# Moving five layer-1 blocks and twelve gathers from a PEER loop into the end of its gate matrix

## The chip, the cores and the metric

The kernel runs on one core of a Trainium2 chip. The metric is the device time of one execution in microseconds (us), lower is better. TensorE is called PE here, VectorE DVE, ScalarE ACT, GpSimd POOL and SyncE SP.

## The reference

One encoder block on 512 tokens of width 1024: normalisation, a combined projection, neighbourhood attention and grouped-query attention, gated merge, residual; then PEER, a retrieval of single-neuron experts; then a last normalisation. The change touches PEER alone:

```python
def peer(xn, w_q, sub_keys, u, v):
    q = (xt @ w_q).reshape(t, PEER_HEADS, 2, PEER_HALF)
    sc = jnp.einsum("thpc,hpnc->thpn", q, sub_keys)
    top_s, top_i = lax.top_k(sc, PEER_TOPK)
    ...
    best_s, best_pos = lax.top_k(cand_s, PEER_TOPK)
    idx = jnp.take_along_axis(cand_i, best_pos, axis=-1)
    gate = jax.nn.softmax(best_s, axis=-1)
    ...
        uc = u[ic]
        act = jnp.einsum("cd,ced->ce", xc, uc)
        hid = jax.nn.gelu(act, approximate=False) * gc
        return jnp.einsum("ce,ced->cd", hid, v[ic])
```

Each token has 8 heads x 16 experts = 128 of the 16384 experts, whose rows of `u` and `v` are 1024 float32 wide.

## The kernel before

The 512 tokens are four tiles of 128. For the first two tiles and half of the third (T1 = 320 tokens) the kernel doesn't gather: it computes all 16384 experts densely, in NK = 128 blocks of 128 experts, and multiplies by a gate matrix that is zero where an expert wasn't chosen. For the other half of the third tile (64 tokens, "X") the products with `u` are gathered row by row, NX = 64 gathers of 128 rows, and the resulting hidden values go through the gate matrix too. The fourth tile (GA) is gathered altogether: P = 128 gathers of u and 128 of v.

A *layer-1 block* (`layer1`, L610) loads one block of `u` (512 KB), splits it into a high part (ACT, `whi`, L82) and a low part (`wlo`, L84, on DVE or POOL), and makes 24 matmuls of 320 columns (L100 to L102) and a Gelu into a tile `ge` of 128 x 320. A *layer-2 block* (`layer2`, L898) makes 18 matmuls of 512 columns (L905) from the hidden values `hh`, `hl` of one block and the split block of `v`, and accumulates in PSUM. `hidden` (L881) multiplies `ge` by the block's gates and splits the product.

The *gate matrix* (L819 to L861) is made from token groups: 96 groups of 4 tokens. For each group DVE writes one-hot tiles `oh` (L838), ACT (odd groups, L844) or POOL (even groups, L846) scales them by the gates, PE multiplies four pairs (L850), and ACT evicts the result into `stg` (L851). Four groups make a chunk, which SP writes to DRAM (`gdram`, L859). The last 16 groups, from group 80 on, need the hidden values of the X half tile: `hx` is transposed on PE and copied to `pk` (L829, L830). Between the groups stand the gathers of X (`gather_x`) and layer-1 blocks.

NB = 47 layer-1 blocks are done ahead of the loop and their `ge` kept in SBUF (pool `blp`): 21 before the gate matrix, NG = 17 spread over the first 80 groups, NP = 5 ahead of `hx`'s transpose, and 4 behind the last gate matmul.

The *loop* (L964) has one step per block: split the next block of v (`vget`), take or make the next block's `ge` (`get_ge`: kept for j < 47, else a layer-1 block in the loop), `hidden`, `layer2`, and some gathers of tile GA (`gather_to`), whose pace is set by `gw`: a step without layer 1 counts 1, one with it 2.25. A gather of u is an indirect DMA that POOL issues (L626, kept in program order) and a multiplication with row sums on DVE (L629); in the X gathers the second factor, `xgx`, lies in PSUM, in those of tile GA, `xg`, in SBUF. A gather of v is an indirect DMA (L634) and a multiply-add on DVE (L637). The pools have few buffers: `raw` 3, `whi` and `wlo` 4 each, `oh` 5, the gather pool of X (`gatx`) 4, those of the loop (`gat`) 3 for u and 3 for v.

The order on each engine is fixed at build time by a planner that simulates the program; `issue_after` keeps an instruction behind another in that simulation.

Of the kernel before, what the change touches and what calls it, by code (L numbers as in the profile page):

```python
# [11 lines left out]
F32 = mybir.dt.float32  # L12
# [10 lines left out]
P = 128  # L23
# [6 lines left out]
NK = 128  # L30
# [3 lines left out]
TD = ND * P  # L34
HB = P // 2
T1 = TD - HB
NB = 47
CH = 16
GJ = 8
NX = 64  # L40
NEG = -1.0e30
WSTART = (0, 64, 192, 256)
KIND = (1, 0, 0, 2)
# [5 lines left out]
def tile_block(ctx, tc, x, out, g1, g2, gfr, gq, gk, w_in, w_a, w_b, w_o, w_q,  # L49
               rpb, keys, u_rows, u_blk, v_blk, rope_c, rope_s, mask, iota):  # L50
    nc = tc.nc
    mm = nc.tensor.matmul
    act = nc.scalar.activation
    vec = nc.vector
# [63 lines left out]
    dp = ctx.enter_context(tc.tile_pool(name="dp", bufs=1, space=DRAM))  # L118
    bdram = dp.tile([H, P, 512], F32, name="bdram")
    gdram = dp.tile([P, TD // CH, P * CH], F32, name="gdram")  # L120
    xdram = dp.tile([ND, P, D], F32, name="xdram")
    def rstd_int(ss, shape, width, p, tag):
        m = p.tile(shape, F32, name="rm" + tag)
        vec.tensor_scalar(out=m, in0=ss, scalar1=1.0 / width, scalar2=EPS, op0=ALU.mult, op1=ALU.add)
        r = p.tile(shape, F32, name="rr" + tag)
        t = p.tile(shape, F32, name="rt" + tag)
        vec.tensor_copy(out=t, in_=m.bitcast(I32))
        vec.tensor_scalar(out=r.bitcast(I32), in0=t, scalar1=-0.5, scalar2=1597463007.0,
                          op0=ALU.mult, op1=ALU.add)
        vec.tensor_scalar(out=m, in0=m, scalar1=-0.5, scalar2=None, op0=ALU.mult)  # L130
        for _ in range(4):
            vec.tensor_tensor(out=t, in0=r, in1=r, op=ALU.mult)
            vec.tensor_tensor(out=t, in0=t, in1=m, op=ALU.mult)
            vec.scalar_tensor_tensor(out=r, in0=t, scalar=1.5, in1=r, op0=ALU.add, op1=ALU.mult)
        return r
# [47 lines left out]
    with ExitStack() as pa:  # L183
# [329 lines left out]
        xg = xa.tile([P, D], F32, name="xg")  # L513
# [83 lines left out]
    codeU = gp.tile([P, P], I32, name="codeU")  # L597
# [12 lines left out]
    def layer1(j, keep, eng):  # L610
        uh, ul = load_split(u_blk[j], eng)
        ps = psm.tile([P, S], F32, name="ps_mm")
        last_l1[0] = acc3(ps[:, :T1], [(uh[:, k * P:(k + 1) * P], ul[:, k * P:(k + 1) * P],
                                        xah[:, k], xal[:, k]) for k in range(KD)])
        ge = keep.tile([P, T1], F32, name="ge")
        with tc.issue_after(last_hi[0].ins) if j < 2 else ExitStack():
            act(ge, ps[:, :T1], AF.Gelu)  # L617
        return ge

    u_src = u_rows  # L620
# [23 lines left out]
    def gather_to(goal):  # L644
        while sum(npu) < min(goal, 2 * P):
            pu, pv = npu
            if pu < P and pu - pv < 32:
                gather_u(pu, gat, codeU, xg, actg)
                npu[0] += 1
                if npu[0] % 16 == 0:  # L650
                    act_g(pu // 16)
            else:
                gather_v(pv)
                npu[1] += 1
# [3 lines left out]
    with pb:  # L658
# [85 lines left out]

        def backlog(n, eng=vec):
            for _ in range(n):
                if nbl[0] < NB:
                    gelu_bl.append(layer1(nbl[0], blp, eng))
                    nbl[0] += 1

# [3 lines left out]
        def gather_x(goal):  # L754
            while len(stt) < min(goal, NX):
                stt.append(gather_u(len(stt), gatx, codeX, xgx, actx))
# [57 lines left out]
        ngr = T1 // 4 - 8  # L814
        nx0 = len(stt)
        gms = []
        NP = 5
        NG = NB - 4 - NP - nbl[0]
        for ch in range(TD // CH):  # L819
            if ch == T1 // CH - 1:  # L820
                act(actx, actx, AF.Gelu)
                for o, z in ((HB, 0), (0, 1)):
                    vec.tensor_tensor(out=hsel(hx[HB:], z), in0=hcol(actx[o:o + HB]),
                                      in1=hcol(gateX[o:o + HB]), op=ALU.mult)
            if ch == T1 // CH:
                with tc.issue_after(gms[-1].ins):
                    backlog(NP, pool)
                with tc.issue_after(last_l1[0].ins):
                    nc.tensor.transpose(pst[:, :P], hx, ident)  # L829
                vec.tensor_copy(out=ijg[GX][:, 2, HB:], in_=pst[:, HB:P])  # L830
            stg = stp.tile([P, P, CH], F32, name="stg", bufs=3)
            for t4 in range(CH // 4):
                t = ch * CH + t4 * 4
                pk = ijg[t // P]
                c = t % P
                oh = stp.tile([P, 2, 4, P], F32, name="oh", bufs=5)
                with tc.issue_after(stt[max(0, len(stt) - 4)].ins):
                    vec.tensor_tensor(out=oh,  # L838
                                      in0=iops.unsqueeze(1).unsqueeze(1).broadcast_to([P, 2, 4, P]),
                                      in1=pk[:, 0:2, c:c + 4].unsqueeze(3).broadcast_to([P, 2, 4, P]),  # L840
                                      op=ALU.is_equal)
                if t4 % 2:
                    for z in range(4):
                        act(oh[:, 0, z], oh[:, 0, z], AF.Copy, scale=pk[:, 2, c + z:c + z + 1])  # L844
                else:
                    pool.tensor_tensor(out=oh[:, 0], in0=oh[:, 0],  # L846
                                       in1=pk[:, 2, c:c + 4].unsqueeze(2).broadcast_to([P, 4, P]), op=ALU.mult)
                ps = psb.tile([P, S], F32, name="ps_s", bufs=3)
                for z in range(4):
                    gm = mm(ps[:, z * P:(z + 1) * P], oh[:, 0, z], oh[:, 1, z], start=True, stop=True)  # L850
                act(stg[:, :, t4 * 4:t4 * 4 + 4].rearrange("p j t -> p t j"),  # L851
                    ps.rearrange("p (t j) -> p t j", t=4), AF.Copy)
                gms.append(gm)
                g = t // 4
                gather_x(nx0 + (NX - nx0) * (g + 1) // ngr)
                if g and NG * min(g + 1, T1 // 4) // (T1 // 4) > NG * min(g, T1 // 4) // (T1 // 4):
                    with tc.issue_after(gms[-2].ins):
                        backlog(1, (vec, pool)[nbl[0] % 2])
            nc.sync.dma_start(gdram[:, ch], stg.rearrange("p j t -> p (j t)"))  # L859
        with tc.issue_after(gm.ins):  # L860
            backlog(NB, vec)  # L861
        px.close()

    psd = ctx.enter_context(tc.tile_pool(name="psd", bufs=1, space=PSUM, reuse_waits="tile"))
# [56 lines left out]
    ge = {}  # L921

    def get_ge(j):
        return gelu_bl[j] if j < NB else layer1(j, dq, vec)

    def finish(tt):
        if tt == GA:
# [32 lines left out]
    vget = lambda j: load_split(v_blk[j], vec, dq)  # L960
    vnx = vget(0)
    nxt = hidden(0, get_ge(0))
    gw = (2 * P) / (NB + 2.25 * (NK - NB - 5))
    for j in range(NK - 1):  # L964
        cur, vcur = nxt, vnx
        vnx = vget(j + 1)
        nxt = hidden(j + 1, get_ge(j + 1))
        if j < NK - 2:
            layer2(j, cur, vcur)
        with tc.issue_after(nxt[2].ins):  # L970
            gather_to(int(gw * (min(j + 1, NB) + 2.25 * max(0, j + 1 - NB))))
    tc.keep_in_program_order(act(warm, warm, AF.Sqrt))
    finish(GA)
    layer2_last((cur, nxt), (vcur, vnx))
# [80 lines left out]
```

## Time and profile before

| | us |
|---|---|
| median of 3 runs | 1695.64 (1693.13 to 1696.81) |
| profiled execution, its own time | 1703.01 |
| its span, first to last instruction | 1701.1 |
| PE busy | 1603.3 |
| DVE busy | 1296.4 |
| ACT busy | 810.1 |
| POOL busy | 776.1 |

Times in the trace count from the start of the span. A busy PE is not PE at its peak: matmuls are pipelined and their ends are modelled, so the distance of their starts is the better measure. A view of groups sums instructions of one line; a window sums each engine over a stretch; the chain of waits follows the work that ended last back from release to release; the timeline shows instructions in order, with the idle time before each in brackets and what ended it.

### The profile page before, as it was taken

The page shows a single profiled execution, that of the slowest core. Times are in us where ns is not written, and L with a number is a line of the kernel's source. Part 1 is how long each engine was busy: PE and PEld are TensorE (multiplying, and loading weights), DVE is VectorE, ACT ScalarE, POOL GpSimd, SP SyncE. Part 2 cuts the span into 40 slices and gives each one's busy share as a digit, 9 for nine tenths or more (in the row PEclk, how much of TensorE's full clock was granted, in tenths as well). Part 3 has the DMA queues.
Part 4 walks back from the last instruction along what each step waited for, and adds up shares of the span by engine and source line. Part 5 has one row for each costly group of instructions (what it writes and reads, how often), then busy time and mean ns, then how long its engine had stood idle before and what let it go on. Part 6 is the DMA issues. An engine that isn't in the chain of part 4 may idle for free.

```text
span 1701.1 us, 25989 instructions
## 1 busy us (share of the span) xinstructions
PE 1603.3 (94%) x9390; PEld 1439.8 (85%) x9390; DVE 1296.4 (76%) x2595; ACT 810.1 (48%) x1523; POOL 776.1 (46%) x653
## 2 busy tenths in 40 slices
PE   8999999998999868889889999999999999999997
PEld 7888988788999758779878888989898989888986
DVE  7266766536799889997568877888888888888875
ACT  5446566434333358787634434443434344434334
POOL 2543221123688977676213433444444445443341
PEclk9989999999999979999999999999999999999999
DMA  7523221323222559997589999999999999999882
GB/s 249 147 57 92 80 70 50 103 91 125 95 94 92 198 190 343 340 341 272 207 271 338 331 326 315 324 338 334 347 345 336 341 350 332 344 347 311 305 304 106
DMA packets 162482, 407.44 MB, mean 240 GB/s; under 512 B 21297, under 2 KB 72881, under 8 KB 159282
## 3 DMA queue, kind: packets, MB, share of 16 engines
q1 hardware_dynamic: 114848, 235.63, 40.2%
q0 software_dynamic: 47360, 169.89, 28.6%
q8 instruction: 74, 1.21, 0.3%
q14 instruction: 54, 0.44, 0.1%
q10 hardware_dynamic: 146, 0.27, 0.0%
HBM read 374.02 MB, written 30.87 MB: 238 GB/s over the span
## 4 chain that ended last, share of the span: by engine, by line
PE 67%; DVE 12%; DMA 8%; ACT 5%; POOL 4%; issue 4%; SPq 0%; DVEq 0%; POOLq 0%; ACTq 0%
PE acc L905 27%; PE ps_mm L100 11%; PE ps_mm L102 11%; PE ps_mm L101 11%; DMA vg<-in_v_blk_dram,codeV 2%; DMA ug<-in_u_rows_dram,codeX 2%; PE ps_s L850 1%; ACT stg L851 1%; POOL wlo L84 1%; DMA raw<-in_v_blk_dram 1%; ACT whi L82 1%; PE ps_o L100 1%; PE ps_o L102 1%; PE ps_o L101 1%; DVE codes L741 1%
## 5 line engine op out<-in xcount | busy, mean ns | idle before, releaser
L82 ACT ACTIVATE whi<-raw 128x1024 fp32r<-128x1024 f32 x322 | 341.4, 1061 | 474.6 <-PE ps_mm L101 202.9
L84 DVE TENSOR_TENSOR wlo<-raw,whi 128x1024 fp32r<-128x1024 f32 x234 | 287.0, 1229 | 144.4 <-ACT whi L82 127.0
L100 PE MATMUL ps_mm<-xah,whi 128*128 128x320 f32 x1152 | 361.7, 314 | 7.5 <-ACT ge L617 5.8
L102 PE MATMUL ps_mm<-xah,wlo 128*128 128x320 f32 x1152 | 359.6, 312 | 6.3 <-POOL wlo L84 3.6
L101 PE MATMUL ps_mm<-xal,whi 128*128 128x320 f32 x1152 | 358.6, 311 | 0.0
L84 POOL TENSOR_TENSOR wlo<-raw,whi 128x1024 fp32r<-128x1024 f32 x88 | 213.1, 2423 | 288.7 <-ACT whi L82 249.6
L626 POOL DMA_INDIRECT ug<-in_u_rows_dram,codeU x128 | 159.1, 1243 | 261.7 <-DVE ug L629 241.8
L634 POOL DMA_INDIRECT vg<-in_v_blk_dram,codeV x128 | 177.6, 1387 | 219.7 <-DVE yg L637 197.4
L905 PE MATMUL acc<-whi,hh 128*128 128x512 f32 x756 | 243.3, 397 | 4.4 <-ACT hh L90 4.4
L905 PE MATMUL acc<-wlo,hh 128*128 128x512 f32 x756 | 239.6, 397 | 0.0
L905 PE MATMUL acc<-whi,hl 128*128 128x512 f32 x756 | 235.0, 395 | 0.0
L100 PEld LDWEIGHTS ps_mm<-xah,whi 128*128 128x128 f32 x1152 | 218.4, 190 | 12.8 <-ACT ge L617 7.2
L102 PEld LDWEIGHTS ps_mm<-xah,wlo 128*128 128x128 f32 x1152 | 218.2, 189 | 8.9 <-POOL wlo L84 4.4
L101 PEld LDWEIGHTS ps_mm<-xal,whi 128*128 128x128 f32 x1152 | 218.4, 190 | 3.6
L637 DVE SCALAR_TENSOR_TENSOR yg<-vg,hidg,yg 128x1024 f32<-128x1024 f32 x128 | 164.2, 1283 | 11.3 <-DMA vg<-in_v_blk_dram,codeV 11.1
L905 PEld LDWEIGHTS acc<-wlo,hh 128*128 128x128 f32 x756 | 142.5, 188 | 34.5
L905 PEld LDWEIGHTS acc<-whi,hl 128*128 128x128 f32 x756 | 142.0, 188 | 34.3
L905 PEld LDWEIGHTS acc<-whi,hh 128*128 128x128 f32 x756 | 139.0, 188 | 32.4 <-ACT hh L90 5.3
L629 DVE SCALAR_TENSOR_TENSOR ug<-ug,xg 128x1024 f32<-128x1024 f32 x128 | 155.7, 1219 | 0.0
L850 PE MATMUL ps_s<-oh 128*128 128x128 f32 x768 | 108.7, 294 | 33.1 <-POOL oh L846 20.0
L850 PEld LDWEIGHTS ps_s<-oh 128*128 128x128 f32 x768 | 100.5, 200 | 39.8 <-POOL oh L846 25.9
L90 ACT ACTIVATE hh<-hd 128x384 fp32r<-128x384 f32 x128 | 66.8, 522 | 140.2 <-DVE hd L892 115.8
(278 smaller groups left out, 2879.8 us busy)
## 6 DMA issues: line engine op xcount, KB each, us to landing
raw<-in_u_blk_dram SPq DMA_DIRECT2D x128, 512.0 KB
raw<-in_v_blk_dram SPq DMA_DIRECT2D x128, 512.0 KB
gdram<-stg SPq DMA_DIRECT2D x24, 1024.0 KB
gtl<-gdram SPq DMA_DIRECT2D x64, 384.0 KB
raw<-in_w_in_dram SPq DMA_DIRECT2D x34, 512.0 KB
raw<-in_w_q_dram SPq DMA_DIRECT2D x16, 512.0 KB
x_t<-in_x_dram SPq DMA_DIRECT2D x8, 512.0 KB
raw<-in_w_o_dram SPq DMA_DIRECT2D x8, 512.0 KB
```

Of the source, the lines that this page charges most:

```text
L82: act(hi, raw, AF.Copy)
L84: eng.tensor_tensor(out=lo, in0=raw, in1=hi.bitcast(F32), op=ALU.subtract)
L90: last_hi[0] = act(hi, src, AF.Copy, scale=scale)
L100: mm(ps, ah, bh, start=i == 0, stop=False)
L101: mm(ps, ah, bl, start=False, stop=False)
L102: last = mm(ps, al, bh, start=False, stop=i == n - 1)
L626: i_ = pool.indirect_dma_start(out=t, out_offset=None, in_=u_src, in_offset=bass.IndirectOffsetOnAxis(ap=code[:, p:p + 1], axis=0))
L629: return vec.scalar_tensor_tensor(out=t, in0=t, scalar=1.0, in1=mul, op0=ALU.mult, op1=ALU.mult, accum_out=dst[:, p:p + 1])
L634: i_ = pool.indirect_dma_start(out=t, out_offset=None, in_=v_src, in_offset=bass.IndirectOffsetOnAxis(ap=codeV[:, p:p + 1], axis=0))
L637: vec.scalar_tensor_tensor(out=yg, in0=t, scalar=hidg[:, p:p + 1], in1=yg, op0=ALU.mult, op1=ALU.add)
L850: gm = mm(ps[:, z * P:(z + 1) * P], oh[:, 0, z], oh[:, 1, z], start=True, stop=True)
L905: mm(accs[tt][hf], st_[:, ts_], mv[:, hf * S:(hf + 1) * S], start=j == 0 and st_ is hh and mv is vh, stop=False)
```

## The change

Five more blocks (NS = 5, numbers 47 to 51) get their layer 1 ahead of the loop. Their `ge` is written to DRAM (`sdram`) by ACT's queue and loaded again in the loop by SP's, two steps ahead. Of the 52 blocks NP = 6 stand ahead of `hx`'s transpose and NA = 8 behind the last gate matmul. NE = 12 gathers of u for tile GA are issued with the last 12 gate groups, 84 to 95, through the X gathers' pool; the loop's pace counts them as done.

```diff
+NS = 5
+NE = 12
...
+    sdram = dp.tile([NS, P, T1], F32, name="sdram")
...
-        ge = keep.tile([P, T1], F32, name="ge")
+        spill = NB <= j < NB + NS
+        ge = stp.tile([P, T1], F32, name="sge", bufs=2) if spill else keep.tile([P, T1], F32, name="ge")
         with tc.issue_after(last_hi[0].ins) if j < 2 else ExitStack():
             act(ge, ps[:, :T1], AF.Gelu)
+        if spill:
+            nc.scalar.dma_start(sdram[j - NB], ge)
...
-                if nbl[0] < NB:
+                if nbl[0] < NB + NS:
...
-        NP = 5
-        NG = NB - 4 - NP - nbl[0]
+        NP = 6
+        NA = 8
+        NG = NB + NS - NA - NP - nbl[0]
...
                 gather_x(nx0 + (NX - nx0) * (g + 1) // ngr)
+                if g >= TD // 4 - NE:
+                    gather_u(npu[0], gatx, codeU, xg, actg)
+                    npu[0] += 1
...
         with tc.issue_after(gm.ins):
-            backlog(NB, vec)
+            backlog(NB + NS, vec)
...
     def get_ge(j):
-        return gelu_bl[j] if j < NB else layer1(j, dq, vec)
+        return gelu_bl[j] if j < NB else ge.pop(j) if j < NB + NS else layer1(j, dq, vec)
+
+    def load_ge(j):
+        if NB <= j < NB + NS:
+            ge[j] = dq.tile([P, T1], F32, name="ge")
+            nc.sync.dma_start(ge[j], sdram[j - NB])
...
-    gw = (2 * P) / (NB + 2.25 * (NK - NB - 5))
+    gw = (2 * P - NE) / (NB + NS + 2.25 * (NK - NB - NS - 5))
     for j in range(NK - 1):
         cur, vcur = nxt, vnx
         vnx = vget(j + 1)
+        load_ge(j + 2)
         nxt = hidden(j + 1, get_ge(j + 1))
         if j < NK - 2:
             layer2(j, cur, vcur)
         with tc.issue_after(nxt[2].ins):
-            gather_to(int(gw * (min(j + 1, NB) + 2.25 * max(0, j + 1 - NB))))
+            gather_to(NE + int(gw * (min(j + 1, NB + NS) + 2.25 * max(0, j + 1 - NB - NS))))
```

## Rows read from the trace of the kernel before

**Rows 1.** The page: busy time, share of the span, instructions.

```profile
PE 1603.3 (94%) x9390; PEld 1439.8 (85%) x9390; DVE 1296.4 (76%) x2595; ACT 810.1 (48%) x1523; POOL 776.1 (46%) x653
```

**Rows 2.** Windows: length, busy of five engines (count), granted clock, DMA share, GB/s.

```profile
799.40:817.30 17.90, 17.83 (x122) 17.56 (x121) 3.71 (x4) 7.74 (x12) 4.83 (x2) 1.00 0.53 182
817.30:843.90 26.60, 20.52 (x139) 19.27 (x140) 19.42 (x18) 24.35 (x50) 12.01 (x11) 0.94 0.48 177
843.90:860.10 16.20, 12.81 (x89) 12.55 (x87) 2.18 (x4) 3.83 (x9) 0.00 (x0) 1.00 1.06 343
...
892.30:1060.00 167.70, 167.70 (x720) 135.01 (x721) 137.71 (x204) 68.54 (x121) 58.50 (x50) 1.00 0.95 326
1060.00:1520.00 460.00, 460.00 (x2510) 411.48 (x2509) 382.29 (x477) 188.34 (x306) 212.46 (x154) 1.00 0.96 340
```

**Rows 3.** Chain that ended last, in order of time: start, length, what.

```profile
843.91 6.80 DMA gdram<-stg
850.77 7.91 DMA gtl<-gdram
...
1067.59 4.20 PE acc L905 x18
1075.31 4.20 PE acc L905 x18
...
1585.22 4.20 PE acc L905 x18
...
1673.59 4.20 PE acc L905 x18
```

**Rows 4.** Timeline of PE, last gate groups and start of the loop.

```profile
838.38 2.26 PE L850 MATMUL ps_s<-oh 128*128 128x128 f32 x16 [0.58 <-ACT oh L844]
841.23 1.36 PE L850 MATMUL ps_s<-oh 128*128 128x128 f32 x8 [0.58 <-ACT oh L844]
...
860.06 0.73 PE L905 MATMUL acc<-whi,hh 128*128 128x512 f32 x2 [3.39 <-ACT hh L90]
...
892.29 0.73 PE L905 MATMUL acc<-whi,hh 128*128 128x512 f32 x2 [1.02 <-ACT hh L90]
```

**Rows 5.** Groups by line, 817.3 to 843.9 us: busy, mean ns, idle before.

```profile
L851 ACT ACTIVATE stg<-ps_s 128x512 f32<-128x512 f32 x16 | 15.4, 1073 | 0.9 <-PE ps_s L850 0.9
L844 ACT ACTIVATE oh<-oh,pk 128x128 f32<-128x128 f32 x32 | 10.1, 399 | 1.3 <-DVE oh L838 1.3
```

**Rows 6.** Windows: the X gathers' stage, and the loop's first 5 us.

```profile
650.00:750.00 100.00, 80.82 (x576) 77.67 (x575) 91.66 (x112) 80.30 (x155) 69.45 (x59) 0.97 0.94 338
860.00:865.00 5.00, 4.94 (x15) 3.91 (x16) 4.96 (x8) 2.97 (x7) 0.94 (x1) 0.66 0.23 45
```

**Rows 7.** Groups by line, 1060 to 1520 us.

```profile
L84 DVE TENSOR_TENSOR wlo<-raw,whi 128x1024 fp32r<-128x1024 f32 x120 | 147.6, 1231 | 43.8 <-ACT whi L82 43.5
L82 ACT ACTIVATE whi<-raw 128x1024 fp32r<-128x1024 f32 x121 | 128.5, 1063 | 196.5 <-PE ps_mm L101 130.7 <-PE acc L905 58.0 <-DMA raw<-in_v_blk_dram 5.5
...
L629 DVE SCALAR_TENSOR_TENSOR ug<-ug,xg 128x1024 f32<-128x1024 f32 x77 | 93.8, 1218 | 0.0
```

**Rows 8.** Instructions of the tile gdram: ns least/median/most, first and last start.

```profile
L877 SPq DMA_DIRECT2D gtl<-gdram x64: 377/430/1823, 844.9 to 1587.9; - x64
```

**Rows 9.** Timeline of all engines, 823 to 842 us, rows of DVE and POOL.

```profile
823.06 1.22 DVE L84 TENSOR_TENSOR wlo<-raw,whi 128x1024 fp32r<-128x1024 f32 x1
...
823.29 1.89 POOL L846 TENSOR_TENSOR oh<-oh,pk 128x512 f32<-128x512 f32 x1 [1.22 <-DVE oh L838]
...
824.20 12.53 DVE L838 TENSOR_TENSOR oh<-ps_t,pk 128x1024 f32<-128x1024 f32 x11
...
835.74 1.04 POOL L846 TENSOR_TENSOR oh<-oh,pk 128x512 f32<-128x512 f32 x1 [1.22 <-DVE oh L838]
...
839.95 0.94 POOL L626 DMA_INDIRECT ug<-in_u_rows_dram,codeU  x1 [0.31 <-issue]
```

**Rows 10.** Gathers of line 626, 628 to 800 us: issue to landing.

```profile
DMA to landing us min/median/max: 4.3/7.0/9.2
```

## Prediction before the run

> **What bounds the kernel now.** I read the page first: TensorE (PE) is busy for 94% of the span [rows 1]. That is an average over unlike stages, so next come the windows around the edit [rows 2]. From 892 to 1520 us PE is busy without a break: 720 matmuls in 167.7 us early on, 0.233 us each, and no idle later. The chain of waits gives the loop's unit prices [rows 3]: the 18 matmuls of one layer-2 block last 4.20 us, and with a layer-1 block beside them the period is 7.72 us. So a layer-1 block costs 3.52 us of PE wherever PE is full, and a block taken out of the loop saves 3.52 us there.
>
> Where PE isn't full is the end of the gate matrix. Between 817.3 and 843.9 us the last 16 of the 96 gate groups run; ACT is busy 24.35 of 26.6 us, PE 20.52 [rows 2]. PE's gaps of 0.58 us recur every two groups, 2.85 us apart, and end with ACT's scaling of `oh` [rows 4]: ACT paces a pair of groups with four scalings and two evictions [rows 5]. Then four layer-1 blocks follow the last gate, PE idles 3.39 us, and the loop begins at 860.06 [rows 4]. What ends last there is a transfer chain: the write of the last gate chunk (6.80 us), then the load of the loop's first gate tile (7.91 us) [rows 3], while the DMA engines move 343 GB/s [rows 2]. After that idle time the granted clock is 0.66 until 865 us, a mixture of its two levels, 1.2 and 2.4 GHz [rows 6]. The seven blocks from 860.06 to the next gap, which begins 1.02 us before 892.29 [rows 4], take 31.2 us in place of 7 x 4.20 = 29.4.
>
> The loop's tail loses a little too. Block starts at 1585.22 and 1673.59 us lie 88.37 us apart [rows 3]; eleven periods would be 84.9, so 3.5 us are lost while the last gathers are waited for.
>
> **The change, part by part.** The blocks paced along the gate groups stay 17: before 47-4-5-21, after 52-8-6-21 (21 are done earlier). So one block joins those ahead of the last 16 groups, four join those behind the last gate, and five leave the loop.
>
> *One block more ahead of the groups.* PE is full there (17.83 of 17.90 us for five blocks, [rows 2]), and the transpose of `hx`, the copy to `pk` and every later `oh` stand behind it: **+3.5 us**. Its subtraction runs on POOL (two in 4.83 us, [rows 2]), which idles there; without that cover it would cost those 2.4 us.
>
> *Four more blocks behind the last gate.* The last gate matmul ends about 842.4 us ([rows 4]: eight matmuls from 841.23), and the loop starts at 860.06, 17.7 us later. Eight blocks need 28.2 us, so the loop starts later by **+10.5**. The transfer chain took 16 us from the last eviction; even lengthened by the new bytes it should now end under these blocks. Their splits (ACT 1.06 us, DVE 1.23, [rows 7]) fit below 3.52 us per block.
>
> *Idle filled.* If PE runs on into the loop, the low clock there goes, and with it 31.2-29.4: **-1.8**.
>
> *Five blocks fewer in the loop.* 5 x 3.52 = **-17.6**. The loads that replace them are five of 160 KB, 0.82 MB, or 2.5 us of the DMA engines at 326 GB/s [rows 2]. On SP each stands behind a load of v and ahead of the next one, and waits for a `ge` buffer used two blocks earlier. But the loop also loses 2.6 MB of u and 6.3 MB of gathers, so I take 0 of 0 to 2.5. The five stores are issued on ACT's queue. None such is in the trace of this stage; an issue of SP lasts 0.43 us [rows 8], and ACT is busy 3.83 of 16.2 us there [rows 2], so 0, or 2.1 if ACT were full.
>
> *Twelve gathers beside groups 84 to 95.* They leave a loop in which PE is the limit, so what they free there (12 x 1.22 us of DVE, 18 us of the DMA engines) buys little. The gathers per late block fall from 2.64 to 2.59, which can ease only the tail: I take **-1.0** of the 3.5 us lost, bounds 0 and -3.5.
>
> Where they go they have a price. POOL works in its own order, with two gathers between two scalings of `oh`. An issue lasts 0.94 us with 0.31 before it, a scaling 1.04 [rows 9]. The sixth scaling before the end ends at 825.2 (823.29 and 1.89, [rows 9]); five more scalings and ten gathers are 5.5 + 12.5 us, so the scaling for group 94 ends at 843.2, where now it ends at 836.8, and the last gate comes near 845.6 instead of 842.4: 3.2 us late though no buffer was short. But `gatx` has four buffers. The fifth gather waits until the first has landed (7.0 us, [rows 10]) and DVE has multiplied it (1.22 us, [rows 7]), so it starts at 833.6, 1.3 us later than its place in the queue; the ninth likewise waits for the fifth, until 841.9. Walked on in that way, scaling 94 ends at 845.2 and the last gate at 847.5: 5.1 us late. The bound from below is 0, if the queue holds the gathers behind the scalings. From above: if DVE does all twelve products ahead of its last `oh`, it has 28 + 1 operations of 1.14 us (eleven in 12.53, [rows 9]) from 817.4; the last ends at 850.5 and the last gate near 852.9, 10.5 us late. The products read two SBUF operands, unlike those of the X gathers, whose second operand is in PSUM. The one scaling that ran beside a two-operand subtraction on DVE took 1.89 us in place of 1.04 [rows 9]; five more of that kind would be 4.3 us, still inside the bound. I take **+5.0**, the walk, since gathers and scalings stand in just that order in the program.
>
> The Trainium skill (SBUF — State Buffer, Who interferes with whom) says that a DVE instruction with two SBUF inputs and a GpSimd instruction that reads SBUF exclude each other, the later one waiting out the whole instruction of the other. By it all five could be held, which would put the sum below at +2.9; the single row at 1.89 agrees with it, but doesn't show how often they meet.
>
> Sum: 3.5 + 10.5 - 1.8 - 17.6 - 1.0 + 5.0 = **-1.4 us**, against the profiled execution's 1703.01 us. That lies 7.4 us over the median of 1695.64; carried over, 1694.2 us. Within 0.2% (3.4 us), about what a measurement of this kernel can tell from no change, that is the same.
>
> **The rivals.** *A: the gate groups are not held up.* POOL's scalings run ahead now (group 94's ends at 836.8, and its matmuls at 840.6, [rows 4, 9]), and the planner may put gathers or products behind the last `oh`. Then the +5.0 goes: -6.4, and with the whole tail regained -8.9. Against it: the transfers. Now 177 GB/s x 26.6 us + 343 x 16.2 [rows 2] = 10.3 MB move between 817.3 and 860.1; twelve gathers (6.3), five u blocks (2.6) and the spills (0.8) make 20.0. At 343 GB/s, with the first three loop gathers (1.6 MB) left for after the start of the loop, that is 53.7 us: from 820.8 to 874.5, against 874.1 for PE. So this case is just feasible; any slack in the transfers is paid.
>
> *B: the gate groups become bound by DVE and POOL.* It is a matter of place on two in-order queues: products ahead of `oh`, and scalings behind gathers that wait. In the stage of the X gathers, 650 to 750 us, DVE is busy 92% of the time [rows 6], so such a mixture has been at its limit before. Price 10.5 us instead of 5.0: +4.1, and with the tail and clock terms gone +6.9. The change loses from 6.4 us of delay on, and shows as slower from 9.8.
>
> *C: the transfer chain still ends last.* Gathers and u loads take the DMA engines from the last chunk's write and the first gate tile, PE idles behind its eight blocks, and the clock falls as now. With 5 us of such idle the sum is +5.4. For it speak the full DMA rows [rows 2]; against it that the chain has 28 us rather than 14 to hide under.
>
> **How the numbers follow.** My forecast (delay 3 to 8 us, -3.4 to +1.6) 0.45; A 0.30; B 0.15; C 0.10. Some of A ends within 0.2% (0.02), some of the forecast's lower end, with more of the tail regained, beyond it (0.06), and a little of B and C inside (0.03). So faster 0.34, same 0.44, slower 0.22. The range goes from about -6 (1689) to +6 (1701.6): the forecast, most of A, and B and C but for their ends.
>
> **What would show it.** Right: the last gate matmul near 851 us and the first layer-2 matmul near 879, with no idle of PE between and a full clock after; the loop's first layer-1 block five blocks later; in groups 84 to 95 PE waiting for POOL's scaling, and POOL for DVE's product. Wrong: if the pairs still take 2.85 us, A holds; if DVE is full from 821 us to the last gate, B; if PE idles ahead of the loop on the gate tile, C. A delay of the last gate other than 5 us makes the prediction wrong by just the difference.

## The result: 12 us slower, where 1.4 us faster was forecast

The changed kernel takes 1708.53 us (median of 20 runs, 1700.21 to 1716.07), the kernel before 1696.22 (20 runs, 1690.87 to 1702.24). The ratio is 1.0071, with a 95% interval of 1.0059 to 1.0083: 10 to 14 us slower, outside the forecast's range.

The profiled execution of the changed kernel took 1703.78 us, 5 under its median, and that of before 1703.01, 7 over its own. Laid side by side the two traces differ by 0.9 us, so each kernel was profiled a second time (before: 1697.87; after: 1705.95). The stages, from the starts of PE's matmuls in the four traces, in us:

| stage | before | 2nd | after | 2nd | forecast | measured (means) |
|---|---|---|---|---|---|---|
| start to first gate matmul | 628.9 | 626.4 | 624.4 | 623.9 | 0 | -3.5 |
| to the transpose of `hx` | 188.1 | 189.3 | 189.6 | 189.2 | +3.5 | +0.7 |
| to the last gate matmul | 25.3 | 24.7 | 29.4 | 29.3 | +5.0 | +4.4 |
| to the first layer-2 matmul | 17.8 | 17.4 | 32.8 | 32.7 | +10.5 | +15.2 |
| loop, to the merged last blocks | 821.0 | 818.2 | 805.2 | 808.5 | -20.4 | -12.8 |
| to the end | 20.0 | 20.0 | 20.6 | 20.6 | 0 | +0.6 |

The first stage has no part of the change in it. In the other kernels below it lasts 622.0 to 628.4 us, so its -3.5 is scatter, and the rest sums to +8.1. Two steps failed: the start of the loop (+15.2 in place of +10.5) and the loop (-12.8 in place of -20.4).

### The profile page after: what moved, and what is told of

Its sections match the earlier page's. It is cut to its first block, busy times and chain, and to the rows that moved or that the text cites. A ratio compares the mean times of both kernels' runs of the same rounds, so it can differ in the third digit from the quotient of the medians.

```text
span 1702.0 us, 26019 instructions
## 1 busy us (share of the span) xinstructions
PE 1594.7 (94%) x9390; PEld 1432.0 (84%) x9390; DVE 1297.7 (76%) x2594; ACT 810.7 (48%) x1523; POOL 784.9 (46%) x654
## 4 chain that ended last, share of the span: by engine, by line
PE 66%; DVE 15%; DMA 7%; issue 5%; POOL 4%; ACT 4%; DVEq 0%; ACTq 0%; POOLq 0%
PE acc L915 24%; PE ps_mm L102 11%; PE ps_mm L104 11%; PE ps_mm L103 11%; DMA raw<-in_v_blk_dram 3%; PE ps_s L857 2%; DMA vg<-in_v_blk_dram,codeV 2%; DVE oh L845 2%; DVE wlo L86 1%; DMA ug<-in_u_rows_dram,codeX 1%; ACT whi L84 1%; POOL wlo L86 1%; POOL eqc L744 1%; PE ps_o L102 1%; PE ps_o L104 1%
## 5 line engine op out<-in xcount | busy, mean ns | idle before, releaser
L915 PEld LDWEIGHTS acc<-whi,hh 128*128 128x128 f32 x756 | 139.1, 188 | 32.8 <-ACT hh L92 5.1
```

The source lines that it names most:

```text
L915: mm(accs[tt][hf], st_[:, ts_], mv[:, hf * S:(hf + 1) * S], start=j == 0 and st_ is hh and mv is vh, stop=False)
```

## The profile after

The page's busy time hardly moves: PE is still busy 94% of the span [rows 1].

```profile
PE 1594.7 (94%) x9390; PEld 1432.0 (84%) x9390; DVE 1297.7 (76%) x2594; ACT 810.7 (48%) x1523; POOL 784.9 (46%) x654
```

The windows answer to [rows 2, 6]: the blocks ahead of the groups, the last 16 groups, the last gate to the loop, the loop's start, and two stretches of the loop.

```profile
796.10:814.00 17.90, 17.90 (x124) 17.90 (x123) 3.67 (x3) 6.91 (x10) 5.80 (x3) 1.00 0.51 171
814.00:843.80 29.80, 20.02 (x133) 18.26 (x132) 25.88 (x29) 24.32 (x49) 19.34 (x17) 0.89 0.73 264
843.80:876.20 32.40, 28.08 (x193) 27.82 (x191) 14.80 (x22) 10.59 (x19) 6.46 (x5) 1.00 0.94 320
875.00:880.00 5.00, 3.83 (x10) 3.02 (x11) 4.75 (x10) 2.18 (x5) 2.55 (x2) 0.66 0.76 232
892.30:1060.00 167.70, 167.70 (x720) 134.81 (x719) 139.55 (x203) 69.21 (x123) 56.47 (x50) 1.00 0.97 334
1110.00:1520.00 410.00, 410.00 (x2236) 366.42 (x2236) 340.64 (x425) 165.85 (x270) 192.47 (x139) 1.00 0.95 338
```

The groups take 29.8 us in place of 26.6, with DVE now the busiest engine. In the third window PE works 28.1 us, just the eight blocks of the forecast, but the window lasts 32.4, while the DMA engines move 320 GB/s at a share of 0.94. After it the granted clock is 0.66 again, as it was in [rows 6].

The timeline of PE, the last gate groups and the start of the loop, against [rows 4]:

```profile
838.95 4.73 PE L857 MATMUL ps_s<-oh 128*128 128x128 f32 x24 [1.36 <-ACT oh L851]
...
876.16 0.90 PE L915 MATMUL acc<-whi,hh 128*128 128x512 f32 x2 [4.32 <-ACT hh L92]
```

PE idles 4.32 us where it idled 3.39. Its chain of waits, against the first lines of [rows 3]:

```profile
861.33 0.45 ACT sge L621
861.79 5.80 DMA sdram<-sge
867.61 6.66 DMA gtl<-gdram
...
875.01 0.50 DVE hd L902
875.59 0.53 ACT hh L92
876.16 2.18 PE acc L915 x5
```

A spill's store, then the gate tile's load. The tile comes in four loads, and the last was issued at 867.61 us, just as that store had landed; the second was issued at 864.08, just as the first spill's store had landed (864.07). In the trace the transfers of SP and ACT share eight semaphores, and each of these two loads waited until the store that had used its semaphore before had landed, though the two share no data. Before, these loads were issued from 844.9 us on [rows 8]. The timeline of SP's queue shows what stands ahead of it now:

```profile
845.06 0.32 SPq L869 DMA_DIRECT2D gdram<-stg  x1
849.45 11.36 SPq L82 DMA_DIRECT2D raw<-in_u_blk_dram  x4
860.91 0.37 SPq L82 DMA_DIRECT2D raw<-in_v_blk_dram  x1
863.62 4.99 SPq L887 DMA_DIRECT2D gtl<-gdram  x4
```

Four loads of u wait there for buffers that PE's blocks give back one by one. And the timeline of ACT shows a second row of work that can't start before the last block has ended:

```profile
871.88 0.44 ACT L621 ACTIVATE sge<-ps_mm 128x320 f32<-128x320 f32 x1 [3.08 <-PE ps_mm L104]
872.35 0.33 ACTq L623 DMA_DIRECT2D sdram<-sge  x1
872.78 1.06 ACT L84 ACTIVATE whi<-raw 128x1024 fp32r<-128x1024 f32 x1 [0.46 <-ACT sge L621]
874.35 0.40 ACT L903 ACTIVATE hd<-gtl 128x64 f32<-128x64 f32 x2 [0.52 <-DMA gtl<-gdram]
875.59 0.94 ACT L92 ACTIVATE hh<-hd 128x384 fp32r<-128x384 f32 x2 [0.83 <-DVE hd L902]
```

The split of the loop's first v stands behind the last gelu; ACT then waits for the gate tile for only 0.52 us. So two chains end almost together, and one of them isn't a transfer.

In the groups the mechanism of the prediction's walk is what happened, with other places: six gathers, not ten, stand on POOL ahead of the scaling of group 94. Waits of PE on POOL's scalings, before from 817.3 to 843.9 us and then after from 814 to 844 us, and of POOL on DVE's products after (total, times, longest):

```profile
PE ps_s L850 <- POOL oh L846: 2.6, 1, 2.6
```

```profile
PE ps_s L857 <- POOL oh L853: 7.7, 6, 2.6
...
POOL ug L632 <- DVE ug L635: 3.0, 3, 1.4
```

The two of POOL's eight scalings that took longer than 1.05 us:

```profile
820.34 1.89 POOL L853 TENSOR_TENSOR oh<-oh,pk 128x512 f32<-128x512 f32 x1 [1.29 <-DVE oh L845]
...
833.61 1.89 POOL L853 TENSOR_TENSOR oh<-oh,pk 128x512 f32<-128x512 f32 x1 [1.17 <-DVE oh L845]
```

One of them ran beside a subtraction and one beside a product, each with two SBUF operands on DVE. By the Trainium skill's rule (SBUF — State Buffer, Who interferes with whom) all that met such an operation were to be held; these two were. Before, one of the eight was held in the same way [rows 9], so the change added one.

## Experiments

All times are medians; the difference is the ratio to the kernel before on the same chip, less one, times 1696 us. The ratios aren't those of the medians, and can lie apart from them: for blocks_vhalf the medians give 1.0020.

| run | us | ratio, 95% interval | difference | last gate to loop | loop |
|---|---|---|---|---|---|
| after_again | 1711.43 | 1.0100 [1.0062, 1.0138] | +17 | 32.7 | 808.5 |
| gathers_only | 1708.25 | 1.0068 [1.0042, 1.0094] | +12 | 26.2 | 823.5 |
| blocks_only | 1713.13 | 1.0097 [1.0072, 1.0121] | +16 | 32.8 | 816.5 |
| np10_na4 | 1714.67 | 1.0114 [1.0088, 1.0141] | +19 | 26.8 | 805.7 |
| all_gtlpool | 1712.37 | 1.0094 [1.0068, 1.0121] | +16 | 36.8 | 805.9 |
| blocks_gtlpool | 1714.46 | 1.0108 [1.0082, 1.0133] | +18 | 33.8 | 816.5 |
| no_spill | 1704.16 | 1.0060 [1.0043, 1.0078] | +10 | 32.2 | 805.6 |
| gathers_early | 1705.04 | 1.0056 [1.0038, 1.0073] | +9 | 15.5 | 818.0 |
| blocks_gtl_v0 | 1710.36 | 1.0071 [1.0054, 1.0088] | +12 | 31.0 | 809.9 |
| blocks_vhalf | 1700.57 | 1.0006 [0.9992, 1.0019] | +1 | 32.7 | 807.5 |
| before_vhalf | 1693.98 | 0.9981 [0.9967, 0.9996] | -3 | 17.1 | 817.1 |
| all_vhalf | 1703.24 | 1.0034 [1.0020, 1.0049] | +6 | 32.8 | 801.0 |
| all_v0 | 1708.92 | 1.0067 [1.0045, 1.0090] | +11 | 34.3 | 809.5 |
| all_gtl_v0 | 1710.13 | 1.0076 [1.0047, 1.0104] | +13 | 33.7 | 808.9 |
| gathers4_early | 1699.20 | 1.0023 [1.0003, 1.0042] | +4 | 17.7 | 818.0 |

### Each half by itself

The first theories were SP's queue (the gate tile behind the u loads) and the held-up groups.

**after_again**: the changed kernel, unedited.

> The changed kernel once more, for a second trace of it, since one execution differs from the next by several us. Both theories: about 12 us over the kernel before. The queue theory (the load of the loop's first gate tile stands on SP behind four u loads, which wait for block splits) expects PE idle for 4 us again right before the loop and the first loop matmuls at the low clock; the groups theory (the gathers hold up the gate groups) expects the last gate about 4 us later after the transpose of hx than before (29 us in place of 25).

**gathers_only**: the twelve gathers without the blocks.

```diff
-NS = 5
+NS = 0
...
-        NP = 6
-        NA = 8
+        NP = 5
+        NA = 4
```

> The twelve gathers beside the last gate groups, but no further layer-1 block (47 blocks, 5 and 4 as before). Groups theory: the last gate comes 4 to 5 us late and nothing gives it back, so +3 to +5 us, and most of the 12. Queue theory: SP's order behind the last gate is that of the kernel before, so the loop starts 18 us after the last gate as before, and of the 12 us only the 4 of the groups are here.

**blocks_only**: the blocks without the gathers.

```diff
-NE = 12
+NE = 0
```

> The five further layer-1 blocks kept in DRAM, but all gathers in the loop. Groups theory: the gate groups take 25 us again, and the blocks pay by filled idle time: -3 to -5 us against the kernel before. Queue theory: the loop's first gate tile still waits on SP behind four u loads, PE idles 4 us before the loop and is cold: +2 to +8 us.

**np10_na4**: ten blocks ahead of the last groups and four behind the last gate.

```diff
-        NP = 6
-        NA = 8
+        NP = 10
+        NA = 4
```

> The whole change, but ten blocks ahead of the transpose of hx and four behind the last gate, in place of six and eight; so no u load stands on SP between the last gate chunk's write and the first gate tile. Queue theory: the idle time before the loop falls back to 3 us or less of pure transfer time and the time lies 4 to 7 us under the changed kernel. Groups theory: the gathers stand where they stood, so within 2 us of the changed kernel.

Neither theory covers these. Each half alone costs as much as the whole. Without gathers the groups take 24.9 us, as before, and yet the time is +16: the groups theory falls as the main cause. With four blocks behind the last gate no u loads stand ahead of the gate tile, and yet the loop starts 26 to 27 us after the last gate: the queue is not all either. The chain of the gathers alone, last eviction to loop:

```profile
839.81 7.76 DMA gdram<-stg
847.64 15.58 DMA gtl<-gdram
```

The chunk's write took 7.76 us (before 6.80) and the tile's load 15.58 (before 7.91) [rows 3], at a DMA share of 1.02 over the 26.2 us (the view counts a packet where it starts, so a share can pass 1). A third theory, bandwidth, came of it. And blocks_only loses in its loop: 126 blocks by 4.20 us and 76 layer-1 blocks by 3.51 are 796 us, the loop took 816.5, 20 more; before, by the same sum with 81 (813.5), it lost 7.5 and 4.7.

### The gate tile out of SP's queue, the spills, and the gathers earlier

**all_gtlpool** and **blocks_gtlpool**: the same line in the whole change, and in blocks_only.

```diff
-        i_ = nc.sync.dma_start(gtile[1][:, cs], gdram[:, cs, n * GJ * CH:(n + 1) * GJ * CH])
+        i_ = (nc.sync if n else pool).dma_start(gtile[1][:, cs], gdram[:, cs, n * GJ * CH:(n + 1) * GJ * CH])
```

> The whole change, but the four loads of the first gate tile are issued on POOL's queue and not on SP's, so they no longer stand behind four u loads and a v load that wait for PE. Queue theory (they came late because of that place): the tile lands earlier, the 4.3 us of idle PE ahead of the loop and the low clock behind it go; 4 to 6 us under the changed kernel, 1703 to 1706 where that is at 1709, still 6 to 8 over the kernel before. Bandwidth theory (the gathers, the u loads and the chunks fill the DMA engines from 825 us on, and the chain ends when the bytes are through): under 2 us gained, and the idle time stays within 1 us of 4.3.

> The blocks without the gathers (which took 1713), with the first gate tile's loads on POOL's queue. Here the DMA engines were busy only 41 to 68% of the time while the tile was late, so both theories give the same sign: the idle time ahead of the loop (4.5 us) and the low clock after it go, 5 to 7 us, to 1706 to 1708. If it is still 10 us or more over the kernel before, the greater part of what the five blocks cost lies in the loop (the trace lost 20.4 us there against 7.3 before): a third cause, in the reload of the gelu tiles or in the pace of the gathers.

**no_spill**: the five gelu tiles neither stored nor loaded.

```diff
-        if spill:
-            nc.scalar.dma_start(sdram[j - NB], ge)
...
-            ge[j] = dq.tile([P, T1], F32, name="ge")
-            nc.sync.dma_start(ge[j], sdram[j - NB])
+            ge[j] = gelu_bl[j - NS]
```

> The whole change without the traffic of the five gelu tiles: they are not stored and not loaded, and the loop takes five earlier tiles in their place (so the output is not the reference's). Spill theory (the stores keep the first gate tile waiting, and the loads on SP hold up the v loads behind them): the loop starts some us earlier and 5 us or more are gained against the changed kernel, to 1704 or less. If the traffic is as free as I predicted, within 2 us of the changed kernel; what is lost is then lost to the place of the u loads, the gathers and the loop's new pace of gathers.

**gathers_early**: gathers_only, with the twelve ahead of the last groups. The edit also gives three of the five blocks' subtractions there to DVE.

```diff
-                    backlog(NP, pool)
+                    for z in range(NP):
+                        backlog(1, (vec, pool)[z % 2])
+                    while npu[0] < NE:
+                        gather_u(npu[0], gatx, codeU, xg, actg)
+                        npu[0] += 1
...
-                if g >= TD // 4 - NE:
-                    gather_u(npu[0], gatx, codeU, xg, actg)
-                    npu[0] += 1
```

> The gathers without the blocks, but the twelve are issued ahead of the last 16 groups, beside the five blocks that PE has there, so most are through the DMA engines before the last chunks are written. Bandwidth theory (in the run with the gathers alone, the last chunk and the first gate tile took 7.8 and 15.6 us in place of 6.8 and 7.9): last gate to loop falls from 26 to 18 to 20 us, and the time to 0 to +3 us against the kernel before. Groups theory (POOL's queue): the gathers now hold the first scalings instead, the delay of the last gate stays 2 us or grows, +4 to +8. If it is still at +10 or more with the loop at 18 to 20 us after the last gate, the loss of the gathers lies in the loop.

In the whole change, moving the tile's loads gained nothing: the loop began 36.8 us after the last gate, and PE idled 8.30 us ahead of it. The gelus of the spilled blocks, on ACT ahead of everything the loop needs, now waited for the stores of two blocks earlier, since `sge` has two buffers (total, times, longest):

```profile
ACT sge L621 <- DMA sdram<-sge: 12.1, 3, 5.0
```

The DMA share is 0.96 from 845 to 860 us and 1.03 from 860 to 875, so that is bandwidth, together with the two buffers; no run has more of them. But in blocks_gtlpool, where the tile's loads were issued by 850.6 us and ACT did not wait for them, PE idled still longer than in blocks_only (4.32), though both theories had expected 5 to 7 us to be gained. Its ACT and its PE:

```profile
870.03 0.44 ACT L621 ACTIVATE sge<-ps_mm 128x320 f32<-128x320 f32 x1 [2.83 <-PE ps_mm L104]
870.50 0.33 ACTq L623 DMA_DIRECT2D sdram<-sge  x1
870.93 2.00 ACT L84 ACTIVATE whi<-raw 128x1024 fp32r<-128x1024 f32 x2 [0.46 <-ACT sge L621]
872.84 0.38 ACT L903 ACTIVATE hd<-gtl 128x64 f32<-128x64 f32 x2
874.87 0.94 ACT L92 ACTIVATE hh<-hd 128x384 fp32r<-128x384 f32 x2 [1.65 <-DVE hd L902]
```

```profile
875.45 1.22 PE L915 MATMUL acc<-whi,hh 128*128 128x512 f32 x2 [5.45 <-ACT hh L92]
```

Gelu, store, two splits of v and the hidden tile's copy run one behind the other on ACT with nothing to wait for but each other, and DVE has the low parts of both splits ahead of `hd`: a cause that no theory had named, ACT's own order. no_spill lies between its two expectations: by the ratios it is 2 us under the first runs of the changed kernel and 7 under after_again, the intervals overlap, and the start of the loop hardly moved (32.2 us after the last gate, where it was 32.8). It settles only that the spills are not the main cause.

gathers_early bears bandwidth out at the start of the loop, and shows its price; its time, +9, lies above what either theory expected. Its chain:

```profile
853.34 5.29 DMA gdram<-stg
858.69 6.64 DMA gtl<-gdram
```

Write and load take 11.9 us in place of 23.3, and the loop starts 15.5 us after the last gate. But the groups now wait: `hx` to last gate is 36.1 us in place of 27.4, with DVE busy 25.00 of 25 us from 820 to 845 and a granted clock of 0.77. From `hx` to the loop it takes 51.6 us with the gathers ahead of the groups and 53.6 with them among the groups, against 43.1 and 42.1 before; and the loop without them (818.0 and 823.5) is no shorter than before.

### ACT's order, and half the bytes of v

**blocks_gtl_v0**: blocks_gtlpool, with the first v split ahead of the last gelus, and the next two behind the first hidden's.

```diff
-            backlog(NB + NS, vec)
+            backlog(NB + NS - nbl[0] - 2, vec)
+            v0[0] = load_split(v_blk[0], vec)
+            v0[1] = hi_i[0]
...
+            backlog(2, vec)
...
-    vnx = vget(0)
+    vnx = v0[0]
...
+        hold[0] = last_hi[0] if j < 2 else None
         vnx = vget(j + 1)
```

> The blocks alone, with the first gate tile's loads on POOL's queue (that run took 1714; its tile was in long before PE ran out, and PE still idled 5.5 us). New here: the first v is loaded and split ahead of the last two of the eight blocks, and the splits of the second and third v stand behind the first hidden's. ACT-queue theory (the gelu of the last block ends 0.4 us after PE, and the first v's split, the next one's, the hidden tile's copy and its split stand behind it on ACT, one after another): the idle time falls from 5.5 to about 2.5 us, and the time by 3 to 4 us. If transfers held PE after all, the idle time stays at 5 us or more. In the loop nothing changes by either theory: some 20 us lost there against 18-matmul blocks at full pace, so the time stays 10 us or more over the kernel before.

**blocks_vhalf** and **before_vhalf**: blocks_only and the kernel before, with half the columns of v loaded in the loop and used twice. They leave out the other half of v.

```diff
-    vget = lambda j: load_split(v_blk[j], vec, dq)
+        nc.sync.dma_start(raw[:, :S], src[:, :S])
+        two = raw[:, :S].unsqueeze(1).broadcast_to([P, 2, S])
...
+        act(z2(hi), two, AF.Copy)
...
+        vec.tensor_tensor(out=z2(lo), in0=two, in1=z2(hi.bitcast(F32)), op=ALU.subtract)
```

> The blocks alone (which took 1713), but each v load in the loop brings half its columns, and both halves of the split are made from that half, so ACT, DVE and PE do the same work on half the bytes (the output is not the reference's). Bandwidth theory of the loop (in the short blocks v, the gate tile and the gathers already fill the DMA engines to 92%, and five more short blocks with the gathers of a shorter loop are held up by late v loads): the 20 us lost in the loop fall to 5 or less and the five blocks give back nearly their 17.6; the time is 12 to 16 us lower, 1697 to 1701. If DVE's queue or the pace of the gathers holds the loop, less than 4 us are gained.

> The kernel before with v loads of half the bytes (the output is not the reference's): the control for the run above. Bandwidth theory: it lost 7 us in its loop and gains 3 to 6, to 1690 to 1693, so the blocks gain on it less than on their own. If transfers don't hold its loop: the same as before within 2 us. If it gains 10 us or more, the loop before was bound by transfers as well, and the change's blocks were never worth 3.52 us each.

**before_2**: the kernel before, unedited.

> The kernel before once more, for its profile. The profiled execution of before took 1703, 7 us over its median, and reached the gate matrix at 628.9 us where the others here reached it between 623.9 and 628.4. If that lay in the front and in the loop, this one reaches the gate matrix near 626 and ends near 1695; then all of the kernels above lose 5 to 6 us more than a comparison with the first trace shows.

ACT's order is shown. The start of the loop in blocks_gtl_v0:

```profile
875.48 0.73 PE L925 MATMUL acc<-whi,hh 128*128 128x512 f32 x2 [2.56 <-ACT hh L96]
```

The idle time falls from 5.45 to 2.56 us, and the time by 0.37%, 6 us, more than the 3 to 4 expected (the two intervals overlap a little). Its loop was 6.6 us shorter too, which the theory didn't ask for. The traces show where: PE's waits from 880 to 1110 us fall from 5.2 to 0.9 us, and the granted clock is 0.83 in place of 0.66 from 874 to 884 us, and 1.00 in place of 0.66 from 1003 to 1008.

The loop's loss is transfers in part. Halved v loads take 15 us off the blocks alone (1.0097 to 1.0006) and 3 off the kernel before: by the ratios some 12 us of what the blocks cost hang on the loads of v, by the medians 10. Waits of PE from 880 to 1680 us, first in the second profile of before, then in blocks_only (total, times, longest):

```profile
PE ps_mm L102 <- DVE wlo L84: 0.9, 2, 0.6
...
PE acc L905 <- ACT hh L90: 0.5, 1, 0.5
```

```profile
PE ps_mm L104 <- DVE wlo L86: 7.0, 11, 1.1
PE acc L915 <- ACT hh L92: 3.4, 2, 3.0
PE ps_mm L102 <- ACT whi L84: 0.7, 1, 0.7
```

Most of these waits are for a low part of u (`ps_mm` is layer 1), and the 11.1 us are of three kinds. Four waits before 1110 us, 5.0 us together, end chains that begin with a late v. The chain of the longest:

```profile
990.45 10.88 DMA raw<-in_v_blk_dram
...
1001.41 1.06 ACT whi L84
1002.47 0.42 ACT hh L92
```

The DMA share is 1.05 while that load is under way. From 1003 to 1008 and from 1105 to 1110 us the granted clock is 0.66, which takes 1.7 us each time; so late v costs some 8 us in this trace. Eight waits of 0.6 us between 1110 and 1600 us, 4.6 us together, don't begin with a transfer. The first, on ACT, DVE and PE:

```profile
1346.74 1.06 ACT L84 ACTIVATE whi<-raw 128x1024 fp32r<-128x1024 f32 x1 [5.09 <-PE ps_mm L103]
```

```profile
1347.84 1.22 DVE L86 TENSOR_TENSOR wlo<-raw,whi 128x1024 fp32r<-128x1024 f32 x1 [2.58 <-ACT whi L84]
```

```profile
1349.12 0.41 PE L104 MATMUL ps_mm<-xah,wlo 128*128 128x320 f32 x1 [0.57 <-DVE wlo L86]
```

The split waits until PE has given back a buffer of `whi`, and the low part then comes too late: that is the order of the program. The first trace of before has one such wait, at 1527.7 us. The remaining 1.4 us lie in the tail. In blocks_vhalf the waits before 1110 us fall to 0.7 us and those up to 1600 to 0.9. But the planner orders each edited program anew, and the eight waits may have gone with the order and not with the bytes; no run separates the two.

ACT's waits for v, 890 to 1060 us, in before_2, blocks_only and blocks_vhalf:

```profile
ACT whi L82 <- DMA raw<-in_v_blk_dram: 63.2, 36, 5.1
```

```profile
ACT whi L84 <- DMA raw<-in_v_blk_dram: 66.1, 35, 6.1
```

```profile
ACT whi L82 <- DMA raw<-in_v_blk_dram: 35.8, 29, 3.5
```

Already before, 36 splits in 170 us waited for their v, and PE stayed full; the blocks alone wait hardly more in sum, but a few loads come too late for PE. before_2 is as expected: gate matrix at 626.4 us, 1697.87.

### The same two causes in the whole change

**all_vhalf**, **all_v0** and **all_gtl_v0**: the edits of blocks_vhalf and of blocks_gtl_v0 on the whole change, the last with the edit of all_gtlpool as well.

> The whole change with v loads of half their columns in the loop (the output is not the reference's). Halving them took 3 us off the kernel before (1694) and some 12 to 15 off the blocks alone (1701). Bandwidth theory of the loop: the whole change, whose trace lost 9 to 12 us in the loop against 4.5 to 7 before, gains 5 to 8 us, to 1700 to 1704, and still stands some 6 to 9 over the halved kernel before, by the idle time ahead of the loop and the held-up gate groups. If it gains as much as before does, 3 us, the loop's transfers are no part of the change's price. If it ends within 3 us of the halved kernel before, they are nearly all of it.

> The whole change with the first v loaded and split ahead of the last two of the eight blocks, and the splits of the second and third v behind the first hidden's; the first gate tile stays on SP behind the u loads. ACT-queue theory alone: the 4.3 us of idle PE ahead of the loop falls to 2 to 2.5, 2 to 4 us gained. Both chains end close together in the changed kernel's trace (ACT waited 0.5 us for the gate tile behind the split of v), so by the transfer theory the tile now ends last and at most 1 us is gained.

> As the run before, and the first gate tile's loads on POOL's queue. With the tile alone moved there, the whole change took 1712 and the last gate to the loop 36.8 us, since the gelus waited 3 times (12 us) for the stores of the spilled tiles in full DMA engines. Bandwidth theory: that stays, last gate to loop 34 to 36 us and the time 1708 to 1712. ACT-queue theory: last gate to loop 31 or less, 1704 or less. Neither theory expects a time under the kernel before.

**gathers4_early**: gathers_early with four gathers.

```diff
-NE = 12
+NE = 4
```

> Only four of the twelve gathers, ahead of the last 16 groups, and none of the blocks: the one piece that the traces leave room for (from 820 to 845 us the DMA engines of the kernel before are busy half of the time, and with twelve gathers out of it the loop lost 4 us in place of 4.5 to 7). Bandwidth theory: four gathers, 2 MB, fit there and leave the transfer chain at 17 to 18 us behind the last gate; 0 to -3 us against the kernel before. Groups theory: DVE's four products (4.9 us) ahead of the first groups hold the last gate up by 2 to 5 us, and the time is +1 to +4.

Halving v takes the whole change from +12 or +17 to +6, that is 6 to 11 us, against 3 for before: the loads of v in the loop are 3 to 8 us of the change's price, by the same experiment and with the same doubt about the order. Putting ACT's order right gains nothing clear of noise here, with the tile on either queue. The chain ahead of the loop in all_v0, and then ACT in all_gtl_v0:

```profile
866.08 8.95 DMA gtl<-gdram
...
875.25 0.50 DVE hd L912
```

```profile
877.89 0.44 ACT L626 ACTIVATE sge<-ps_mm 128x320 f32<-128x320 f32 x1 [4.97 <-DMA sdram<-sge]
878.36 0.33 ACTq L628 DMA_DIRECT2D sdram<-sge  x1
```

In all_v0 the gate tile ends last; in all_gtl_v0 it is the store of a spilled tile, which holds the last gelu for 4.97 us. The DMA share from 860 to 875 us there is 0.97 to 1.04. So in the whole change the idle time hangs on transfers, whichever is put ahead; whether more buffers for `sge` would take this last wait away was not run.

Four gathers gain nothing: the loop is 818.0 us with them moved (before_2: 818.2), and DVE's products hold the last gate up by some 2 us. No version here beats the kernel before.

## Why the prediction was wrong

**The groups (+5.0)**: right, +4.4, by the mechanism walked through; 3.7 of it is PE's longer wait on `oh` (9.8 us in place of 6.1). That six gathers and not ten stood ahead of the last scaling was not foreseen. **The block ahead of `hx` (+3.5)**: +0.7 in the means, but this stage scatters; with six blocks ahead of `hx` it lasts 188.9 to 191.5 us in eleven traces, with five 185.7 to 190.0 in six, 2.2 less in the mean, and the four further blocks of np10_na4 (202.5) add 3.1 each. So 3.5 was a little high.

**The start of the loop (+10.5) and the idle filled (-1.8)**: the failing step is "even lengthened by the new bytes it should now end under these blocks". I gave the chain 28 us to hide under and did not look at where its load would stand. Four u loads, each waiting for a block of PE, went ahead of it on SP; four more blocks brought 2 MB of u into the same stretch; and the first v's split fell behind the last gelu on ACT, an order that no term had. It measured +15.2, and the clock stayed at 0.66. Case C, with a chance of 0.10, was this one; its price of +5.4 covers what lies ahead of the loop, and not what the loop itself lost.

**The loop (-17.6, and -1.0 in its tail)**: the failing step is that "a layer-1 block costs 3.52 us of PE wherever PE is full, and a block taken out of the loop saves 3.52 us there". The cost is right; the saving isn't. The loop measured -12.8 in the whole change and, against the mean of both traces of before, -3.1 in blocks_only. What the runs show in its place is PE waiting in the loop, 11.1 us in blocks_only, where the two traces of before have 3.7 and 2.3 in the same stretch: for late v and the low clock behind it (some 8 us), and in eight waits that come of the order (4.6). The rows that show PE full show the DMA engines at 0.95 and 0.96 beside it [rows 2], and from them a bound can be estimated. Five blocks less are 17.6 us less of DMA time, at 330 GB/s 5.8 MB; they take 2.6 MB of u away and bring 0.8 MB of gelus back. So 4.0 MB, 12 us, had no place if the engines were full all the time; the two shares leave some 27 of the 628 us free, so that is an upper bound. The prediction had no such term. With the twelve gathers (6.3 MB) gone from the loop as well, it is 9.7 us shorter than in blocks_only and falls short of -17.6 by 5 us; the eight waits aren't there either, so the bytes alone needn't have done it. The tail gave nothing back: from 1590 to 1678 us PE waits 3.7 and 3.0 us for low parts in the two traces of after, 2.1 and 0.3 in those of before. And the gathers were moved into a stretch that the change filled as well. Before, the DMA engines were free for 52% of the 26.6 us of the groups [rows 2], 13.8 us or, at 343 GB/s, 4.7 MB; the change brought 9.7 MB to that stretch and the next one, which was already full (1.06). I wrote down that sum in case A, 53.7 us of transfers that end at 874.5 against 874.1 for PE, and took it as "just feasible". It needed every queue to issue at the right time.

**What stays open.** The stages without the first sum to +8.1, the medians say +12.3. The results list the mean granted clock: 0.9845 over 82 timed runs of before and 0.9817 over 20 of after, while the profiled executions of after had 0.986 and 0.984. Among the runs of one kernel a clock lower by 0.001 goes with 0.9 to 1.1 us, so some 3 us of the gap may be executions with more or longer stretches at the lower level; that is argued from the lists, not shown in a trace. After the halved v, blocks_vhalf is still 4 us above before_vhalf by the ratios, 7 by the medians; 15.6 us at the start of the loop and 9.6 gained in it account for most of that. Why the loop gains 9.6 rather than 17.6 there is open in part: from 1600 us on PE waits 4.7 us for low parts of u in blocks_vhalf and 1.4 in before_vhalf, and the profiled execution of blocks_vhalf was the slowest of its twelve.

## What to carry to other kernels

A stage in which PE is full and the DMA engines are at 95% has two bounds: before work is taken out of it, count the bytes that leave with each microsecond. Bytes and blocks that are moved into a gap bring their queues with them, so write out each engine's order there, ACT's last evictions included, and ask what the next stage's first instruction stands behind. When both halves of a change lose alone, look for the resource that they share.

## What the runs showed of the hardware

The rows show how much the DMA engines move when they are full: 308 to 351 GB/s in stretches of 15 us and more at a share of 0.94 or over, with 423 at most in 5 us of np10_na4. The Trainium skill (DMA: Bandwidth & Descriptors, Specifications) gives about 358 GB/s as a core's part of HBM and 435 as the fabric's ceiling; the longer stretches agree with the first, and the short peak lies between the two. Unexpected was how far the time of a single load varies among full DMA engines: the last issue of the gate tile, 384 KB, took 6.64 us with the gathers early, 7.91 before, and 15.58 with the gathers late, at shares of 1.04, 1.06 and 1.02. So the share doesn't tell how long one load will take.
